# First rows of a fused encoder layer in another fixed order, with three weight casts on GpSimd

## The chip, the cores and the metric

The kernel runs on one core of one Trainium2 chip. The metric is the device time of one launch in microseconds (us), a median over runs. The core's engines have a queue each and work through it in order: TensorE (PE, with its weight loads listed as PEld), VectorE (DVE), ScalarE (ACT), GpSimd (POOL) and SyncE (SP), which issues most of the DMAs.

## The reference

One layer on x (512 rows of 1024 float32): a root-mean-square norm and an input product, two mixers side by side (a state-space scan and a spatial gate), a gated merge, cross-attention to a 256-row memory, and a SwiGLU feed-forward part. What matters here is how it begins:

```python
def rms_norm(x, g):
    xf = x.astype(jnp.float32)
    y = xf * lax.rsqrt(jnp.mean(xf * xf, axis=-1, keepdims=True) + EPS)
    return (y * g.astype(jnp.float32)).astype(x.dtype)
...
        n = rms_norm(h, mix_norm_g[i])
        proj = n @ w_in[i]
        xa = proj[..., :OFF_U]
        zu = proj[..., OFF_U:OFF_V]
        zv = proj[..., OFF_V:OFF_GA]
```

## The kernel before

Every large product is made of three TensorE products. An operand x is split into hi, x rounded to TensorE's float32r format (`F32R`), and lo = x - hi. `mm3` (L421) then accumulates hi times hi, hi times lo and lo times hi into one PSUM bank. So each weight block and each activation costs a cast (the hi half) and a subtraction (the lo half) before it can be multiplied. In most of the kernel `split` (L83) does this, with the cast on ACT and the subtraction on DVE.

The weights come in blocks in a fixed plan. SP loads the raw blocks into three buffers ahead of use. The first product of the kernel is the first half of the columns `zv`: 512 columns, 1024 input rows, in four weight blocks of 256 input rows each. Block w is loaded as `raw[w]`, and its half k is 128 input rows by 512 columns. Blocks 0 and 1 are loaded by two DMAs each, block 2 by one.

The 512 rows of x are four tiles t = 0 to 3 of 128 rows. L640 to L650 load the norm's gain, the two halves of tile 0 (one over ACT's queue, one over SP's), and then over SP's queue weight block 0, tile 1, weight blocks 1 and 2, and tiles 2 and 3.

What follows is the part that the change touches: `first_rows` (L661). It runs a list of steps written out by hand, `ORDER` (L728). Each step issues one instruction, or a small group, and pins it: on each engine, the pinned instructions stand in the order of the list. Instructions of the rest of the kernel that are not pinned are placed between them by a planner, which goes by times that it estimates. A wait in one step holds everything behind it on its engine. The steps, with their first digit the row tile t or the weight block w, are:

- `sq` (ACT): the sum of squares of one half row; the two halves of a row are two steps. `ms` (DVE): the first half's sum divided by D, plus epsilon. `rt` (ACT): the square root over the second half's sum, with `ms` as its bias. `rc` (DVE): the reciprocal.
- `pg` (PE): spreads the gain over the partitions, into PSUM. `sc` (DVE): one half row scaled by the reciprocal and the gain, in place.
- `pt` (PE): four transposes of a half row into PSUM. `hi` (ACT) and `lo` (DVE): the two halves of the transposed row's split.
- `whi` (ACT) and `wlo` (DVE): the split of one half k of weight block w. After `wlo01` the load of weight block 3 is issued (L714).
- `p` (PE): `p` t w k is one `mm3`, three matmuls of 128x512, into the PSUM bank of tile t.
- `idle` (PE): products of a tile of ones that nobody reads.

Half row q = 0 feeds weight blocks 0 and 1, half row q = 1 feeds blocks 2 and 3. `ORDER` has 18 of the 32 products of this stage. What is left of blocks 0 to 2 and the whole of block 3 follow in L1164 to L1177, with four groups of transposes for the state-space part set between them (L785, L793).

Before `ORDER` the kernel issues four idle products and loads ACT's function table for the square root (L634 to L636).

Of the kernel before, what the change touches and what calls it, by code (L numbers as in the profile page):

```python
# [9 lines left out]
F32 = mybir.dt.float32  # L10
# [7 lines left out]
P = 128  # L18
D = 1024
# [5 lines left out]
EPS = 1e-6  # L25
# [27 lines left out]
def hybrid_layer_kernel(  # L53
# [490 lines left out]
    mhalf = cp.tile([P, 9], F32, name="mhalf")[:, 0:1]  # L544
    nc.vector.memset(mhalf, -0.5)

# [107 lines left out]

    def first_products(t, w, k):
        ts = slice(t * P, (t + 1) * P)
        kk = 2 * w + k
        hi, lo = first_w[w]
        mm3(pt[t], (xn_hi[:, kk, ts], xn_lo[:, kk, ts]), (hi[:, k], lo[:, k]), kk == 0, False, turn=pinned[0])

    def first_rows():  # L661

        sums, roots, facs, turned = {}, {}, {}, {}
# [5 lines left out]
        def sq(t, i):  # L669
            if i == 0:  # L670
                sums[t] = np_.tile([P, 2], F32, tag="ss", name="ss", bufs=2)
            j = i if t else 1 - i
            sum_sq(sums[t][:, i:i + 1], xt[:, t, HALF[j]])
# [5 lines left out]
        def rt(t):  # L679
            in_order(nc.scalar.activation(sums[t][:, 0:1], sums[t][:, 1:2], AF.Sqrt, bias=roots.pop(t), scale=1.0 / D))  # L680
# [27 lines left out]

        def wlo(w, k):
            in_order(nc.vector.tensor_tensor(first_w[w][1][:, k], raw[w][:, k], first_w[w][0][:, k].bitcast(F32),  # L710
                                             ALU.subtract))
# [8 lines left out]
        steps = {"pg": pg_, "sq": sq, "ms": ms, "rt": rt, "rc": rc, "sc": sc, "pt": tr, "hi": hi, "lo": lo,  # L720
                 "whi": whi, "wlo": wlo, "p": first_products, "idle": idles, "bank": lambda n: bank3()}
# [1394 lines left out]
```

## Time and profile before

| | |
|---|---|
| time, median of 3 runs | 861.02 us (859.04 to 861.72) |
| the profiled execution's own time | 858.73 us |
| its span, first to last instruction | 857.0 us |
| PE busy | 849.1 us, 99% of the span |
| DVE busy | 667.3 us, 78% |
| ACT busy | 468.5 us, 55% |
| POOL busy | 93.9 us, 11% |
| mean granted TensorE clock | 0.998 |

A row of the timeline has the start in us, the length in us, the engine, the line, the operation, what it writes and reads with shapes, and the number of merged instructions; in brackets stands the idle time of the engine ahead of it and what ended that. Lengths of neighbours overlap, since the next instruction is begun before the last one has quite ended. The distance from start to start is then the price in a queue, and the length is what a waiting engine sees. A row of the windows view has the length of a stretch, each engine's busy time in it, the granted clock, the DMA engines' busy share and GB/s.

### The profile page before, as it was taken

Reading aid. Unit: us, or ns where it says so; the run is one execution under the profiler, and the core shown is the slowest. Engines: PE = TensorE matmul, PEld = TensorE weight load, DVE = VectorE, ACT = ScalarE, POOL = GpSimd, SP = SyncE. Lnnn points to the kernel's source line nnn. Section 1 sums busy time; section 2 is a strip of 40 time slices with the busy share of each in tenths; the row PEclk is TensorE's granted clock in tenths of the full one; section 3 lists DMA queues with packets and bytes.
Section 4 is the critical chain, followed back from the end, with each engine's and each line's share of the span. In section 5 each row is a group of like instructions: output and inputs, shape, how many; then the busy total and the mean of one; then the engine's idle time right before and its main releaser. Section 6 shows DMA issues by size and latency. Waiting matters only on the chain.

```text
span 857.0 us, 14705 instructions
## 1 busy us (share of the span) xinstructions
PE 849.1 (99%) x5736; PEld 763.1 (89%) x5736; DVE 667.3 (78%) x1082; ACT 468.5 (55%) x703; POOL 93.9 (11%) x123
## 2 busy tenths in 40 slices
PE   9999999999999999999999999999999999999997
PEld 6888888888889988899899888999999999988886
DVE  7998798899646767578758755888877768898876
ACT  7835843344455534467457554655545555656674
POOL 0003102111022110120010101002111111000000
PEclk9999999999999999999999999999999999999999
DMA  9879467888475798947686745488989897366564
GB/s 270 222 252 253 130 184 165 223 204 217 125 216 178 243 309 261 306 137 212 220 272 183 180 145 134 145 231 218 239 222 237 216 247 187 102 192 208 194 190 159
DMA packets 119480, 176.37 MB, mean 206 GB/s; under 512 B 9665, under 2 KB 83537, under 8 KB 119250
## 3 DMA queue, kind: packets, MB, share of 16 engines
q1 hardware_dynamic: 96370, 143.13, 50.7%
q0 software_dynamic: 22176, 30.64, 22.1%
q10 hardware_dynamic: 864, 1.66, 0.5%
q8 instruction: 45, 0.74, 0.3%
q14 instruction: 25, 0.20, 0.1%
HBM read 166.52 MB, written 52.92 MB: 256 GB/s over the span
## 4 chain that ended last, share of the span: by engine, by line
PE 95%; DMA 2%; DVE 2%; issue 0%; SPq 0%; ACT 0%; ACTq 0%; DVEq 0%
PE pf L424 22%; PE pt L424 17%; PE px L1316 14%; PE pq L1316 7%; PE dx L424 5%; PE dq L424 5%; PE pv L1316 4%; PE bx L1316 3%; PE qx L1316 3%; PE dv L424 2%; PE pz L1018 2%; PE bq L1316 1%; PE po L424 1%; PE psc L424 1%; PE qq L1316 1%; PE qv L1316 1%
## 5 line engine op out<-in xcount | busy, mean ns | idle before, releaser
L85 ACT CAST whi<-wraw 128x1024 fp32r<-128x1024 f32 (+1 forms) x145 | 149.5, 1031 | 171.4 <-PE pf L424 61.4
L86 DVE TENSOR_TENSOR wlo<-wraw,whi 128x1024 fp32r<-128x1024 f32 (+1 forms) x145 | 173.1, 1195 | 60.7 <-ACT whi L85 59.8
L424 PE MATMUL pf<-xn,whi 128*128 128x512 f32 x448 | 139.2, 391 | 0.0
L424 PEld LDWEIGHTS pf<-xn,whi 128*128 128x128 f32 x448 | 83.7, 188 | 16.8
L1316 PE MATMUL px<-fn,whi 128*128 128x256 f32 x512 | 88.8, 277 | 0.0
L424 PE MATMUL pf<-xn,wlo 128*128 128x512 f32 x224 | 87.7, 392 | 0.0
L1316 PEld LDWEIGHTS px<-fn,whi 128*128 128x128 f32 x512 | 77.3, 188 | 0.2
L1316 PE MATMUL px<-fn,wlo 128*128 128x256 f32 x256 | 70.8, 276 | 0.0
L86 DVE TENSOR_TENSOR wlo<-b,whi 128x1024 fp32r<-128x1024 f32 x39 | 47.7, 1222 | 23.4 <-ACT whi L85 23.4
L85 ACT CAST whi<-b 128x1024 fp32r<-128x1024 f32 x39 | 41.1, 1053 | 41.6 <-PE px L1316 25.5
L1316 PE MATMUL pq<-s,whi 128*128 128x256 f32 x352 | 60.5, 276 | 0.0
L1316 PEld LDWEIGHTS pq<-s,whi 128*128 128x128 f32 x352 | 52.9, 188 | 0.0
L424 PEld LDWEIGHTS pf<-xn,wlo 128*128 128x128 f32 x224 | 42.1, 188 | 8.8 <-issue 0.2
L86 DVE TENSOR_TENSOR wlo<-t,whi 128x1024 fp32r<-128x1024 f32 x30 | 36.7, 1224 | 15.1 <-ACT whi L85 14.9
L1316 PE MATMUL pq<-s,wlo 128*128 128x256 f32 x176 | 48.5, 276 | 0.0
L1316 PEld LDWEIGHTS px<-fn,wlo 128*128 128x128 f32 x256 | 48.1, 188 | 0.0
L85 ACT CAST whi<-t 128x1024 fp32r<-128x1024 f32 x30 | 31.6, 1053 | 30.3 <-DVE t L206 11.2
L424 PE MATMUL pt<-whi,xn 128*128 128x512 f32 x128 | 43.5, 403 | 0.0
L424 PE MATMUL dx<-whi,s 128*128 128x512 f32 x132 | 41.3, 389 | 0.0
L424 PE MATMUL dq<-whi,s 128*128 128x512 f32 x122 | 38.0, 389 | 0.0
L1316 PEld LDWEIGHTS pq<-s,wlo 128*128 128x128 f32 x176 | 33.0, 188 | 0.0
L1316 PE MATMUL px<-s,whi 128*128 128x256 f32 x176 | 30.7, 276 | 0.0
(461 smaller groups left out, 2177.9 us busy)
## 6 DMA issues: line engine op xcount, KB each, us to landing
wraw<-in_w_in_dram SPq DMA_DIRECT2D x34, 512.0 KB, 5.5
dsum<-in_w_down_dram SPq DMA_DIRECT2D x20, 512.0 KB, 6.3
wraw<-dsum SPq DMA_DIRECT2D x20, 512.0 KB, 4.2
b<-in_w_gate_dram SPq DMA_DIRECT2D x15, 512.0 KB, 5.0
wraw<-in_w_down_dram SPq DMA_DIRECT2D x15, 512.0 KB, 3.8
b<-in_w_up_dram SPq DMA_DIRECT2D x14, 512.0 KB, 5.8
dsum<-in_w_down_dram POOLq DMA_DIRECT2D x10, 512.0 KB, 8.2
dsum<-dsum POOLq DMA_DIRECT2D x10, 512.0 KB, 6.2
```

The source lines that it names most:

```text
L85: hi = nc.scalar.copy(dst_hi, src)
L86: lo = nc.vector.tensor_tensor(dst_lo, src, dst_hi.bitcast(F32), ALU.subtract)
L424: m = nc.tensor.matmul(ps, a[x], b[y], start=start and i == 0, stop=stop and i == 2, skip_group_check=free)
L1018: nc.tensor.matmul(ps[:, g, :], wt[:, g, :], u[:, o * GO + g, :], start=True, stop=True)
L1316: m = nc.tensor.matmul(ps[:, j, :], a[x], b[y], start=start and j == k == i == 0, stop=k == 3 and i == 2, skip_group_check=True)
```

## The change

The list of steps is replaced by another list with the same 18 products. Three of the first six weight casts (`01`, `10` and `21`) go from ACT to GpSimd, as a new step `pwhi`. Tiles 1 to 3 have one squaring of the whole row, a new step `sqw`, in place of two of half a row with an `ms`; their square root then takes a constant epsilon as its bias. The squares themselves, which nobody reads, go to a tile `dump`, which takes one of the two buffers that the gains use. The four idle products ahead of the first real product are dropped, and the two ahead of the first transposes stay. Since tile 0 now begins with the product `p001`, the first product into a bank is found by a set rather than by its number. The load of weight block 3 is still issued after `wlo01`.

```diff
-    mhalf = cp.tile([P, 9], F32, name="mhalf")[:, 0:1]
+    small = cp.tile([P, 9], F32, name="small")
+    mhalf, eps = small[:, 0:1], small[:, 1:2]
     nc.vector.memset(mhalf, -0.5)
+    nc.vector.memset(eps, EPS)
...
+    begun = set()
+
     def first_products(t, w, k):
         ts = slice(t * P, (t + 1) * P)
         kk = 2 * w + k
         hi, lo = first_w[w]
-        mm3(pt[t], (xn_hi[:, kk, ts], xn_lo[:, kk, ts]), (hi[:, k], lo[:, k]), kk == 0, False, turn=pinned[0])
+        mm3(pt[t], (xn_hi[:, kk, ts], xn_lo[:, kk, ts]), (hi[:, k], lo[:, k]), t not in begun, False, turn=pinned[0])
+        begun.add(t)
...
-            j = i if t else 1 - i
-            sum_sq(sums[t][:, i:i + 1], xt[:, t, HALF[j]])
+            sum_sq(sums[t][:, i:i + 1], xt[:, t, HALF[1 - i]])
+
+        def sqw(t):
+            sums[t] = np_.tile([P, 2], F32, tag="ss", name="ss", bufs=2)
+            if not dump:
+                dump.append(np_.tile([P, D], F32, tag="gain", name="dump", bufs=2))
+            in_order(nc.scalar.activation(dump[0], xt[:, t], AF.Square, accum_out=sums[t][:, 1:2]))
...
         def rt(t):
-            in_order(nc.scalar.activation(sums[t][:, 0:1], sums[t][:, 1:2], AF.Sqrt, bias=roots.pop(t), scale=1.0 / D))
+            in_order(nc.scalar.activation(sums[t][:, 0:1], sums[t][:, 1:2], AF.Sqrt, bias=roots.pop(t, eps), scale=1.0 / D))
...
+        def pwhi(w, k):
+            in_order(nc.gpsimd.tensor_copy(first_w[w][0][:, k], raw[w][:, k]))
...
     ORDER = """
-        pg0 sq00 sq01 ms0 pg1 rt0 whi00 rc0 sc00 sc01 idle2 pt00 whi01 wlo00 pt01 hi00 hi01 lo00 idle4 sq10 wlo01
-        p000 whi10 ms1 p001 lo01 whi11 wlo10 sq11 wlo11 p010 rt1 whi20 rc1 sc10 p011 whi21 wlo20 pt10 sq20 wlo21
-        p020 hi10 ms2 sq21 lo10 p021 sc11 p100 rt2 sq30 rc2 pt11 sc20 p101 sq31 ms3 sc21 pt20 rt3 p110 hi20 rc3
-        sc30 pt21 hi11 p111 lo20 hi21 pt30 lo11 p200 hi30 lo21 p120 sc31 p201 lo30 pt31 bank3 p300 hi31 p210
-        lo31 p301 p211 p121
+        sq00 pg0 pwhi01 pwhi10 sq01 pg1 ms0 rt0 rc0 sc00 idle2 whi00 pt00 hi00 wlo00 sc01 wlo01 sqw1 rt1 lo00 wlo10 pt01
+        p001 whi11 rc1 sc10 p000 sc11 p010 whi20 pt10 hi01 hi10 wlo11 pt11 pwhi21 lo10 wlo20 sqw2 lo01 rt2 hi11 p011
+        p100 rc2 wlo21 lo11 sqw3 p101 p020 rt3 sc20 p110 p121 rc3 sc30 p111 pt20 hi20 sc21 p021 pt30 hi30 sc31 pt21
+        hi21 lo20 p120 pt31 lo30 p201 lo21 p200 hi31 bank3 p300 p301 p211 lo31 p210
     """
```

More of the change, by code (lines that the diff above doesn't have):

```diff
@@ L658, in first_products @@
         hi, lo = first_w[w]
-        mm3(pt[t], (xn_hi[:, kk, ts], xn_lo[:, kk, ts]), (hi[:, k], lo[:, k]), kk == 0, False, turn=pinned[0])
+        mm3(pt[t], (xn_hi[:, kk, ts], xn_lo[:, kk, ts]), (hi[:, k], lo[:, k]), t not in begun, False, turn=pinned[0])
+        begun.add(t)
     def first_rows():
-        sums, roots, facs, turned = {}, {}, {}, {}
+        sums, roots, facs, turned, dump = {}, {}, {}, {}, []
         raw = [plan[i][3].pop("raw") for i in range(3)]
@@ L718, in bank3 @@
             pt[3] = bank("pt3")
-        steps = {"pg": pg_, "sq": sq, "ms": ms, "rt": rt, "rc": rc, "sc": sc, "pt": tr, "hi": hi, "lo": lo,
-                 "whi": whi, "wlo": wlo, "p": first_products, "idle": idles, "bank": lambda n: bank3()}
+        steps = {"pg": pg_, "sq": sq, "sqw": sqw, "ms": ms, "rt": rt, "rc": rc, "sc": sc, "pt": tr, "hi": hi, "lo": lo,
+                 "whi": whi, "pwhi": pwhi, "wlo": wlo, "p": first_products, "idle": idles, "bank": lambda n: bank3()}
         pinned[0] = True
```

## The prediction

> **What bounds the kernel now.** I read the head of the page first, then the windows, then the timeline of the start.
>
> ```profile
> span 857.0 us, 14705 instructions
> PE 849.1 (99%) x5736; PEld 763.1 (89%) x5736; DVE 667.3 (78%) x1082; ACT 468.5 (55%) x703; POOL 93.9 (11%) x123
> ```
>
> PE is idle for 857.0 - 849.1 = 7.9 us of the span. The windows say where.
>
> ```profile
> 5.00:10.00 5.00, 4.70 (x29) 3.41 (x27) 4.62 (x11) 4.24 (x10) 0.00 (x0) 1.00 0.99 371
> 10.00:15.00 5.00, 4.30 (x20) 3.05 (x21) 4.63 (x11) 4.50 (x13) 0.00 (x0) 1.00 1.05 289
> 15.00:20.00 5.00, 5.00 (x31) 4.26 (x31) 4.87 (x10) 3.57 (x9) 0.00 (x0) 1.00 1.01 239
> 100.00:200.00 100.00, 100.00 (x651) 85.64 (x650) 91.08 (x254) 42.86 (x62) 15.12 (x21) 1.00 0.75 193
> 850.00:857.00 7.00, 1.32 (x12) 1.12 (x10) 2.16 (x6) 2.29 (x7) 0.00 (x0) 0.80 0.39 150
> ```
>
> The columns after the length are PE, PEld, DVE and ACT. Up to 15 us PE waits here and there, then it is full until the tail. So the kernel's time is the moment S from which PE runs without a gap, plus the PE work left at S, plus the tail. Only S and the work done ahead of it can change by this edit. The DVE and ACT columns, 4.6 and 4.2 to 4.5 of 5 us, say that these two engines, which make PE's operands, have hardly any room before 15 us either.
>
> PE's own rows around S, with the idle products at 7.31 (two passes each, so eight rows for four):
>
> ```profile
> 6.20 1.27 PE L694 MATMUL ptr<-ident,xt 128*128 128x128 f32 x8 [0.30 <-DVE pows L819]
> 7.31 1.06 PE L632 MATMUL pt<-ones 128*128 128x128 f32 x8
> 8.13 0.47 PE L424 MATMUL pt<-whi,xn 128*128 128x512 f32 x1
> 10.30 0.50 PE L424 MATMUL pt<-wlo,xn 128*128 128x512 f32 x1 [0.30 <-DVE wlo L710]
> 12.05 0.66 PE L694 MATMUL ptr<-ident,xt 128*128 128x128 f32 x4 [0.31 <-DVE xt L688]
> 14.86 0.63 PE L694 MATMUL ptr<-ident,xt 128*128 128x128 f32 x4
> 16.02 0.60 PE L694 MATMUL ptr<-ident,xt 128*128 128x128 f32 x4
> 21.77 0.27 PE L764 MATMUL plam<-ident,lrows 64*128 64x64 f32 x1
> 25.06 0.61 PE L785 MATMUL pbc<-ident,brow 128*128 128x128 f32 x4
> ```
>
> S is 14.86, at `pt11`. By then 7 of the 18 products of the list are done; 11 products and five groups of transposes (`pt11`, `pt20`, `pt21`, `pt30`, `pt31`) are left. From 14.86 to 16.02 PE does one group and one product: 1.16 us. The 18th product ends at 25.06, where the state-space part's transposes begin, and a small transpose of that part (21.77, 0.2 to the next matmul) stands in between. So 25.06 - 14.86 - 0.2 = 10.0 = 5 x 1.16 + 6 products: a product is 0.70, a group 0.46.
>
> Why S is so late, by the chain of waits, where DMA is a row tile's load:
>
> ```profile
> 4.54 7.51 DMA xt<-in_x_dram
> 12.07 0.72 ACT sq L550 x2
> ...
> 13.37 0.69 DVE xn L703
> ```
>
> Tile 2 lands at 12.05. `hi10`, whose transposes were issued at 12.05, stands behind `sq20` on ACT; `lo10` and `sc11` follow on DVE, and `pt11` waits for `sc11`.
>
> **The change part by part.** Prices of the steps on ACT and DVE:
>
> ```profile
> 5.56 1.29 ACT L707 CAST whi<-wraw 128x512 fp32r<-128x512 f32 x2 [0.55 <-DMA wraw<-in_w_in_dram]
> 8.14 0.63 ACT L550 ACTIVATE sq<-xt 128x512 f32<-128x512 f32 x1
> 10.92 1.12 ACT L707 CAST whi<-wraw 128x512 fp32r<-128x512 f32 x2
> 23.95 1.03 ACT L85 CAST whi<-wraw 128x1024 fp32r<-128x1024 f32 x1
> 5.31 0.75 DVE L688 SCALAR_TENSOR_TENSOR xt<-xt,r,pg 128x512 f32<-128x512 f32 x1
> 7.49 0.69 DVE L703 TENSOR_TENSOR xn<-ptr,xn 128x512 fp32r<-128x512 f32 x1
> 11.05 0.17 DVE L684 RECIPROCAL r<-ss 128x1 f32<-128x1 f32 x1 [0.20 <-ACT ss L680]
> 11.25 0.75 DVE L688 SCALAR_TENSOR_TENSOR xt<-xt,r,pg 128x512 f32<-128x512 f32 x1
> 11.91 1.29 DVE L710 TENSOR_TENSOR wlo<-wraw,whi 128x512 fp32r<-128x512 f32 x2
> ```
>
> On ACT a cast takes 0.62 and its neighbour starts 0.5 later (1.12 for two), a half-row square 0.64 with its read-out. On DVE `rc` takes 0.20 to the next start, `sc` 0.66, and `wlo` 0.61 (1.29 for two of 0.68); I take 0.60 for `lo`.
>
> When data land: the second cast of the pair at 5.56 starts at 5.56 + 1.29 - 0.62 = 6.23, so `raw[0]`'s second half is there by then, and tile 1 by 8.14. For `raw[1]`'s first half, SP's row of its issue and the DMA view of that issue alone (KB, us from issue to landing):
>
> ```profile
> 2.99 1.51 SPq L146 DMA_DIRECT2D wraw<-in_w_in_dram  x3
> wraw<-in_w_in_dram SPq DMA_DIRECT2D x1, 256.0 KB, 5.8
> ```
>
> It lands at 8.79. These loads keep their queue and place, and I leave them where they are.
>
> *The casts on GpSimd* (`pwhi`). The trace has no copy of this size on POOL. Its nearest rows:
>
> ```profile
> 1.49 0.28 POOL masks.py:199 TENSOR_SCALAR_AFFINE_SELECT ident<-ident 128x128 f32<-128x128 f32 x1
> L561 POOL TENSOR_TENSOR r<-ms,mhalf 128x1 f32<-128x1 f32 x10 | 9.1, 910 | 37.9 <-DVE ms L560 37.9
> L886 POOL MEMSET bd<- 128x256 f32 x2 | 0.6, 312 | 0.0
> L2102 POOL MEMSET const-float32-1.0<- 128x1 f32 x1 | 0.1, 104 | 0.0
> ```
>
> From below, twice the memset of 128x256, which reads nothing: 0.62. From the side, the select, which reads and writes: (0.28 - 0.10) / 128 = 1.4 ns per element, so 0.10 + 512 x 0.0014 = 0.82. From above, the same slope on the base of a one-column power, 0.91: 1.63. I take 0.82, since the select is the row that does what a copy does. By the Trainium skill's GPSIMD Engine Reference, section 3.1, a tight loop over 512 elements measured 769 ns; by that, taken as an estimate, the sum below would be 0.05 us better, and no run here shows it yet.
>
> *The new path to S*, step by step. `sc00` ends as before at 6.06. `whi00` (5.56) ends at 6.18, so `wlo00` runs at 6.22 and `sc01` at 6.83; before, `sc01` came first, at 6.06. `pt01` follows `sc01` at 7.6 instead of 6.8. `pwhi01` runs from 6.23 to 7.05; `wlo01` at 7.49, `lo00` at 8.10 to 8.79. `p001`'s first matmul goes at about 8.05 (`p000` went at 8.13), and its last waits 0.3 for `lo00`. Dropping the idle products costs and saves nothing: they ran while PE waited for operands, and this wait remains.
>
> DVE's next step `wlo10` waits for `pwhi10`, which waits for the load: 8.79 + 0.82 = 9.61, `wlo10` at 9.65. Behind it on DVE stand `rc1` (10.26; tile 1's square and root on ACT, 8.14 + 1.05 + 0.3, are done by then), `sc10` (10.46), `sc11` (11.12 to 11.87). On PE `p010`'s second matmul waits for `wlo10` (10.38), `pt10` for `sc10` (11.25), and `pt11` for `sc11`: 11.92. The next, `p011`, has `wlo11` from 11.78 to 12.46 and needs it at about 12.65. So S moves from 14.86 to 11.92, but with only `p001`, `p000` and `p010` done: 15 products are left instead of 11.
>
> Does PE stay full from there? The closest steps on DVE: `lo10` ends at 13.08 and is wanted at 13.5, `lo01` at 14.3 for 14.9, `lo11` at 15.7 for 16.3, `sc20` at 16.3 for 17.2. All arrive, by 0.2 to 0.9 us. Tile 2 (12.05) is no longer ahead of a needed cast: `hi10` stands before `sqw2`.
>
> *One square per row.* The cast of 1024 columns against 512 adds 0.41, so `sqw` is 0.64 + 0.41 = 1.05 in place of two of 0.64, and three `ms` go from DVE. ACT gains 3 x 0.23 and loses three casts of 0.5 to 0.6; none of it ends a wait on the path above, where DVE waits for the load and POOL. I count 0; if ACT were late at `hi10` by more than the 0.4 that `lo10` has spare, it would show there. `eps` is one memset of a column at the start, under the loads: 0. The `dump` tile shares the gains' two buffers; the next tiles there, those of the spatial gate (L1213, L1216), come in the code behind this whole stage: 0. The raw buffers come free as before, so the later loads start as before.
>
> *Sum.* (11.92 - 14.86) + (15 - 11) x 0.70 = -2.94 + 2.80 = -0.14 us. What precedes S moved by almost as much as the work that it used to hold. Against the profiled execution's 858.73 that is 858.6; this execution lies 2.3 us under the median of the three runs, and on the median the forecast is 861.02 - 0.14 = 860.9. Since every 0.1 us more on `pwhi10` moves `wlo10`, `sc11` and S alike, the price of the cast goes straight into the sum: 0.62 gives -0.34, 1.63 gives +0.67.
>
> **The rivals.**
>
> *The GpSimd cast is the new bound (slower).* A row for POOL's one-column power of 0.91 us speaks for a high fixed price per instruction; the memsets of 0.10 and the select of 0.28 speak against it. From 0.96 us per cast the sum is positive: DVE and, behind it, `sc10`, `sc11` and PE wait for `pwhi10`. At 1.63 it is 861.7; to pass +0.3% (2.6 us) the cast would have to take 0.82 + 0.14 + 2.6 = 3.6 us.
>
> *The two engines hold each other up.* No row shows it: POOL has nothing to read at the start. If `pwhi01`, ready at 6.23, and `wlo00`, ready at 6.22, excluded each other, either `pwhi01` would end at 7.72 and `wlo01` run at 7.76 instead of 7.49, which DVE's wait for the load (from 8.70) hides, or `wlo00` would run at 7.10 and `wlo01` at 8.37 to 9.05, and then hold `pwhi10` for 0.26. So 0 to +0.26 beside the sum, 860.9 to 861.1. The Trainium skill's page SBUF — State Buffer, section "SBUF: two separate sides", states such a lock: a DVE instruction with two SBUF inputs and a GpSimd one that reads SBUF do not run together.
>
> *The front shrinks further.* PE's waits ahead of S by my steps are 0.7 for `pt01`, 0.3 in `p001`, 0.3 in `p010`, 0.5 for `pt10` and 0.2 for `pt11`. If the first half of `raw[1]` lands 1 us earlier (tile 1, issued just ahead of it, is there at 8.14) or the cast takes 0.3, then `wlo10` follows `lo00` at 8.75, and `rc1` waits only for tile 1's root, until 9.55 instead of 10.26: -0.7 - 0.14 = -0.8, so 860.2. For it: nothing in this part but this wait is late; against: the issue order of the loads is the same, and DMA is busy 0.99 of the stretch.
>
> *PE's clock falls* with the idle products gone. The first eight idle passes took twice as long as those at 7.31:
>
> ```profile
> 1.06 2.08 PE L632 MATMUL pt<-ones 128*128 128x128 f32 x8 [1.06 <-DVE ones L543]
> 11.00:12.00 1.00, 0.74 (x4) 0.28 (x2) 0.92 (x3) 1.00 (x3) 0.00 (x0) 1.00 0.96 364
> ```
>
> Against it: at 11 to 12 us PE was busy 0.74 and the products after them still went at the 0.70 above. If three products went at twice that, 2.1 more, less the 1.0 of waits that they fill: +1.1 - 0.14 = +1.0, so 862.0.
>
> *The planner sets the rest otherwise*, since its estimated times move: a later load or cast slips behind another on an in-order queue. The closest is block 3:
>
> ```profile
> 25.73 1.23 DVE L86 TENSOR_TENSOR wlo<-wraw,whi 128x1024 fp32r<-128x1024 f32 x1 [0.32 <-issue]
> ```
>
> Its subtraction ends at 26.96. From 25.06 PE has six products of blocks 0 to 2 left (4.2 us), so it is wanted after 29.3 at the earliest: 2.3 us to spare. Either sign, up to 3 us.
>
> **How the numbers follow.** Forecast 0.52, a slow cast 0.16, the lock 0.08, a shorter front 0.12, the clock 0.05, the planner 0.07. A change under 0.3%, 2.6 us, is about what a measurement of this kernel can't tell from none; the three runs before alone span 2.7 us. Only the planner's case passes it by itself, but a median of runs that scatter so can add 1 to 2 us to the outer cases: faster 0.14, same 0.74, slower 0.12. The range takes the cases from -0.8 to +1.0 and the runs' scatter of about 2 us on either side: 858.0 to 863.2.
>
> **What would show it.** In the profile after: a POOL cast of 0.6 to 1.0 us; `wlo10` on DVE at 9.65, right after the second POOL cast; PE's first gapless group at 11.9; then 15 products and five groups, and the 18th product ending within 0.5 us of 24.9. Wrong would be: a first gap of PE after 12.5 us, products more than 0.3 us apart per matmul, a POOL cast above 1.6, or a wait of PE later on that the profile before doesn't have.

## The result, and the profile after

The changed kernel takes 863.09 us (median of 19 runs, 860.09 to 868.1). The kernel before, on the same chip, takes 859.98 us (19 runs, 858.75 to 863.11). The ratio is 1.0028, with a 95% interval of 1.0018 to 1.0039. By the ratio the change made the kernel slower by about 2.4 us; the two medians differ by 3.1 us. The forecast was no change. The profiled execution took 864.44 us, 1.35 us above its median.

The head of its page and two windows of the start (columns as before):

```profile
span 862.6 us, 14678 instructions
PE 850.9 (99%) x5728; PEld 763.9 (89%) x5728; DVE 666.7 (77%) x1080; ACT 465.4 (54%) x694; POOL 96.3 (11%) x126
```

```profile
5.00:10.00 5.00, 3.85 (x21) 2.52 (x19) 4.14 (x10) 3.29 (x7) 1.23 (x2) 1.00 1.00 367
10.00:15.00 5.00, 4.78 (x25) 3.48 (x24) 4.65 (x11) 4.24 (x9) 0.62 (x1) 1.00 0.97 335
```

PE's idle time is 862.6 - 850.9 = 11.7 us, against 7.9 before, and PE was busy 1.8 us more with 8 matmuls fewer. Up to 10 us PE is emptier than before, from 10 us fuller. The front did what it was to do. Its rows in the timeline:

```profile
10.95 1.38 PE L704 MATMUL ptr<-ident,xt 128*128 128x128 f32 x8
12.08 0.48 PE L424 MATMUL pt<-whi,xn 128*128 128x512 f32 x1
24.34 0.27 PE L776 MATMUL plam<-ident,lrows 64*128 64x64 f32 x1
9.35 0.69 DVE L723 TENSOR_TENSOR wlo<-wraw,whi 128x512 fp32r<-128x512 f32 x1 [0.59 <-POOL whi L720]
6.81 0.61 POOL L720 CAST whi<-wraw 128x512 fp32r<-128x512 f32 x1 [5.03 <-DMA wraw<-in_w_in_dram]
8.70 0.62 POOL L720 CAST whi<-wraw 128x512 fp32r<-128x512 f32 x1 [1.28 <-DMA wraw<-in_w_in_dram]
```

`pt10` and `pt11` are the eight transposes at 10.95. This view merges them; in the trace the first transpose of `pt11` starts at 11.70, 0.38 us ahead of the product at 12.08: that is S. The same matmul stands 0.43 us earlier than before all the way from 28 to 90 us.

Where is the time lost, then? The table gives how much later the same matmul of PE starts than in the profile before (median over 5 us from the time at the head), then the median of the runs, that of the kernel before on the same chip, and the ratio of the two. The kernels are those of the experiments below; `before_again` and `after_again` are further runs of the two kernels themselves.

```
                  28     100    400    420    470    520    545   median  before  ratio [95%]
before_again     +0.35  +0.35  +0.35  +0.47  +2.05  +2.05  +2.05  860.92  860.63  1.0008 [0.9997, 1.0018]
before_root2     +0.37  +0.37  +0.37  +0.54  +0.54  +0.54  +0.54  859.44  860.60  0.9992 [0.9980, 1.0004]
before_lam_ctrl  +0.47  +0.42  +0.47  +0.50  +2.07  +2.07  +2.07  860.52  860.45  1.0004 [0.9993, 1.0016]
before_lam_late  +0.47  +2.05  +2.12  +2.03  +2.07  +2.07  +2.07  861.43  860.45  1.0010 [1.0002, 1.0019]
after            -0.43  +1.92  +1.97  +2.29  +3.86  +3.87  +5.61  863.09  859.98  1.0028 [1.0018, 1.0039]
after_again      -0.29  +2.15  +2.19  +2.76  +2.76  +2.76  +5.36  864.03  860.45  1.0041 [1.0021, 1.0060]
after_root2      -0.22  +1.93  +1.97  +2.81  +2.81  +2.81  +2.81  861.97  860.60  1.0024 [1.0008, 1.0041]
after_keep1      +0.01  +0.64  +0.65  +0.63  +0.63  +0.63  +2.44  861.67  859.98  1.0022 [1.0010, 1.0034]
keep1_root2      +0.34  +3.57  +3.57  +3.17  +4.74  +4.74  +4.74  859.96  859.98  1.0012 [0.9993, 1.0032]
after_pow0       +0.71  +0.67  +0.72  +0.51  +2.08  +2.08  +2.42  860.42  860.38  1.0000 [0.9989, 1.0012]
pow0_root2       -0.12  +0.11  +0.16  +0.22  +1.79  +1.80  +1.80  860.47  860.38  0.9993 [0.9983, 1.0003]
lam_early        +0.18  +0.10  +0.10  +0.02  +0.06  +0.06  +1.45  860.40  860.45  1.0004 [0.9991, 1.0018]
lam_keep_late    +0.60  +3.57  +3.57  +3.49  +3.52  +3.53  +5.12  862.16  859.98  1.0029 [1.0017, 1.0041]
lam_act          +1.15  +1.13  +1.13  +1.11  +1.11  +1.11  +1.51  861.38  860.63  1.0007 [0.9994, 1.0021]
lam_sq           +1.24  +1.16  +1.16  +1.08  +1.11  +1.12  +1.12  860.50  860.63  0.9998 [0.9987, 1.0009]
lam_exp          +0.43  +0.38  +0.37  +0.57  +0.57  +0.57  +1.82  859.75  860.63  0.9991 [0.9980, 1.0003]
exp_root2        +0.45  +0.39  +0.38  -0.01  -0.01  -0.00  -0.00  859.67  860.60  0.9992 [0.9981, 1.0003]
```

In the changed kernel's profile two losses belong to the change: 2.4 us between 95 and 99 us (-0.46 at 90, +1.92 at 100), and 1.7 us at 527 us. The 1.6 us between 420 and 470 us do not: they are in one of the two profiles of the changed kernel and in one of the two of the kernel before. A third and smaller loss, 0.3 to 0.8 us between 400 and 420 us, stands in the three profiles `after`, `after_again` and `after_root2`, where PE waits for a `wlo` near 408 us; it is at most 0.2 us in all others, `after_pow0` among them, and was not followed. The view of PE's waits from 20 us to the tail, which is empty for the kernel before, names the places (the last row is the one near 408 us):

```profile
PE ptr L587 <- DVE xs L578: 1.5, 1, 1.5
PE pw L1023 <- DVE zh L1036: 1.1, 1, 1.1
PE pz L1030 <- ACT wt L1024: 0.5, 1, 0.5
PE pt L424 <- DVE wlo L86: 0.4, 1, 0.4
```

**The first loss.** `pw` and `pz` belong to the state-space part, `zt` and the one-column powers to the spatial gate's norm. After, in the order of the chain:

```profile
86.34 0.15 DVE L1219 TENSOR_SCALAR ms<-ms 128x1 f32<-128x1 f32 x1
82.38 1.18 POOL L336 DMA_DIRECT2D bsum<-in_w_proj_b_dram  x1 [7.72 <-DMA bsum<-in_w_proj_b_dram]
88.33 1.17 POOL L336 DMA_DIRECT2D bsum<-in_w_proj_b_dram  x1 [4.77 <-DMA bsum<-in_w_proj_b_dram]
89.00 1.12 POOL L1220 TENSOR_TENSOR r<-ms,small 128x1 f32<-128x1 f32 x1
90.15 0.16 DVE L1221 TENSOR_TENSOR nm<-nm,r 128x1 f32<-128x1 f32 x1 [2.40 <-POOL r L1220]
90.34 1.25 ACT L1222 ACTIVATE zt<-zt,nm,r 128x1024 f32<-128x1024 f32 x1 [2.48 <-DVE nm L1221]
93.00 0.58 ACT L1024 COPY wt<-pw 128x512 f32<-128x512 f32 x1
93.48 1.25 ACT L1222 ACTIVATE zt<-zt,nm,r 128x1024 f32<-128x1024 f32 x1
94.62 0.58 ACT L1024 COPY wt<-pw 128x512 f32<-128x512 f32 x1
96.51 1.04 ACT L1035 COPY zh<-pz 64x512 f32<-64x512 f32 x1
97.58 1.02 DVE L1036 COPY zh<-pz 64x512 f32<-64x512 f32 x1 [0.58 <-ACT zh L1035]
98.66 0.66 PE L1023 MATMUL pw<-ident,wsx 128*128 128x128 f32 x4 [1.12 <-DVE zh L1036]
```

Before, GpSimd's rows of the same stretch:

```profile
78.50 1.18 POOL L336 DMA_DIRECT2D bsum<-in_w_proj_b_dram  x1 [4.70 <-DMA bsum<-in_w_proj_b_dram]
80.75 0.56 POOL L1208 TENSOR_TENSOR r<-ms,mhalf 128x1 f32<-128x1 f32 x1 [1.07 <-DVE ms L1207]
84.17 1.19 POOL L336 DMA_DIRECT2D bsum<-in_w_proj_b_dram  x1 [2.85 <-DMA bsum<-in_w_proj_b_dram]
```

Before, the gate's first power stands between two accumulating loads of `bsum` on GpSimd's in-order queue. After, it stands behind the second one, which waits for its plain load and starts at 88.33. The power's operand was there at 86.34 + 0.15 = 86.5, but it runs at 89.00, 2.5 us later. Its normalization goes to ACT at 90.34, after 2.48 us of idle time, and ACT's queue behind it is late: the second `wt` copy, then `zh`, then DVE's half of `zh`, for which PE waits.

The load itself also comes 4.2 us later than before (88.33 against 84.17), since SP issues its plain load 4.1 us later. On SP's in-order queue that load stands behind stores of what the state-space part has made (`kd<-ks`), and these are as much later. Before, then after:

```profile
75.18 1.83 SPq L970 DMA_DIRECT2D kd<-ks  x4
77.54 1.17 SPq L335 DMA_DIRECT2D bsum<-in_w_proj_b_dram  x1
```

```profile
79.26 1.84 SPq L982 DMA_DIRECT2D kd<-ks  x4
81.64 0.56 SPq L335 DMA_DIRECT2D bsum<-in_w_proj_b_dram  x1
```

So SP's queue carries lateness to GpSimd too. This is read from the rows, and no edit tested it alone; in `before_lam_ctrl`, which loses nothing here, the load is issued at 80.90.

**The second loss** is the same pattern, with the accumulating load of `t` (L199). After, then before:

```profile
528.52 0.15 DVE L562 TENSOR_SCALAR ms<-ms 128x1 f32<-128x1 f32 x1
529.96 1.32 POOL L199 DMA_DIRECT2D t<-in_w_gate_dram  x1 [4.53 <-ACT full L597]
530.80 1.06 POOL L563 TENSOR_TENSOR r<-ms,small 128x1 f32<-128x1 f32 x1
531.90 1.42 DVE L578 SCALAR_TENSOR_TENSOR xs<-h,r,g_f 128x512 f32<-128x512 f32 x2 [3.23 <-POOL r L563]
```

```profile
523.28 1.32 POOL L199 DMA_DIRECT2D t<-in_w_gate_dram  x1 [1.73 <-issue]
524.96 0.56 POOL L561 TENSOR_TENSOR r<-ms,mhalf 128x1 f32<-128x1 f32 x1 [0.35 <-DVE ms L560]
```

Here the order on GpSimd is the same in both kernels, but after, the accumulating load starts later than the power's operand is ready (528.52 + 0.15), and the power follows it by 0.84 us. Before, the load was there 1.68 us ahead of the power, so it had 1.68 - 0.84 = 0.84 us to spare. The row names ACT's `full` as what ended the load's wait, but it cannot be: in the kernel before the load ran at 523.28, ahead of ACT's `full` of that row tile:

```profile
524.84 1.07 ACT L595 COPY full<-ptr 128x512 f32<-128x512 f32 x2 [0.42 <-PE ptr L585]
```

The semaphore events of the trace show the rest. GpSimd's queue ends its wait for the plain load of `t` (and for a semaphore of PE, which had come earlier), and the accumulating load starts 1.2 us behind that in every profile. These are the times, the first less PE's shift at 518 us, beside what PE lost at 527 us:

```
                 wait over  load starts  second power  wait over less shift  lost at 527
before             522.06     523.28       524.96            522.06            0.00
before_again       524.58     525.81       527.01            522.53            0.00
before_lam_ctrl    524.70     525.92       527.03            522.63            0.00
before_lam_late    524.82     526.05       527.03            522.75            0.00
lam_sq             524.23     525.46       526.30            523.11            0.00
after_pow0         525.51     526.74       527.59            523.43            0.33
lam_act            524.62     525.84       526.69            523.51            0.40
lam_exp            524.93     526.16       527.00            524.36            1.25
lam_early          524.57     525.80       526.65            524.51            1.39
lam_keep_late      528.23      529.46       530.31            524.70            1.59
after              528.73     529.96       530.80            524.87            1.75
after_keep1        525.55      526.78       527.63            524.92            1.81
after_again        528.48     529.71       530.56            525.72            2.60
```

Up to 523.1 nothing is lost, and beyond that nearly each us of lateness is one of PE.

### The profile page after: what moved, and what is told of

Read it like the earlier page. It is cut to its first block, busy times and chain, and to the rows that moved or that the text cites. A ratio compares the mean times of both kernels' runs of the same rounds, so it can differ in the third digit from the quotient of the medians.

```text
span 862.6 us, 14678 instructions
## 1 busy us (share of the span) xinstructions
PE 850.9 (99%) x5728; PEld 763.9 (89%) x5728; DVE 666.7 (77%) x1080; ACT 465.4 (54%) x694; POOL 96.3 (11%) x126
## 4 chain that ended last, share of the span: by engine, by line
PE 88%; DVE 5%; DMA 3%; issue 2%; ACT 1%; POOL 1%; SPq 0%; POOLq 0%; DVEq 0%
PE pf L424 21%; PE px L1328 14%; PE pt L424 13%; PE pq L1328 7%; PE dx L424 5%; PE dq L424 5%; PE pv L1328 3%; PE bx L1328 3%; PE qx L1328 3%; PE dv L424 2%; DMA ed<-e 2%; PE qq L1328 1%; PE psc L424 1%; PE qv L1328 1%; PE bq L1328 1%
```

## The experiments

**Is it the lambda transpose?** The transpose `plam` opens the setup of the state-space part, and no step of the list pins it. Before, the planner put it between two products at 21.77. After, it stands behind the list's last product at 24.34, and DVE, which takes the result over, is idle until 24.21:

```profile
24.21 1.23 DVE L86 TENSOR_TENSOR wlo<-wraw,whi 128x1024 fp32r<-128x1024 f32 x1 [2.58 <-ACT whi L85]
25.36 0.22 DVE L778 COPY slab<-plam 128x64 f32<-128x64 f32 x1
```

In the kernel before that copy ran at 22.08, and the chain behind it began at 23.58 instead of 25.61. First theory (A): this delay reaches PE at 95 us. Four kernels, the first being the changed kernel once more. The others pin the transpose and the copy by a new step `lam0`, which also issues the transpose's loads:

```diff
+    def lam(n):
...
+        in_order(nc.tensor.transpose(ps.rearrange("p i g -> p (i g)"), lrows.rearrange("r d p -> r (d p)"), ident[:2 * G, :2 * G]))
+        lr, li = small(), small()
+        in_order(nc.vector.tensor_copy(slab[:, used[0] - 2:used[0], :], ps))
```

`lam_early` has the changed list with `p300 lam0 p301`, `before_lam_late` the old list with `lam0` at its end, and `before_lam_ctrl` the old list with `p300 lam0 hi31`, one matmul behind the planner's place.

> The changed kernel once more, for which of its losses come back. Theory A (a late state-space setup: the small transpose plam now stands behind all 18 products of the list, at 24.3 us instead of 21.8, so VectorE's chain of state-space work starts later and PE waits for it between 60 and 100 us): the loss of about 2.4 us there comes back in the trace, the time is 2 to 3.5 us over the kernel before. The further losses of the first profile (0.3 at 408 us, 1.6 from slower products between 424 and 465, 1.7 at 528 where GpSimd is held) are of that one execution and stay away. Theory B (these later losses belong to the new order of the whole program): they come back too, with about the same sizes.

> The changed kernel, with the loads, the transpose and the copy of plam as a pinned step of the list, behind p300 (PE at about 21.3 us). Theory A: VectorE's state-space chain starts at about 22.5 instead of 25.6 us, PE's wait near 95 to 99 us goes, the time is 0.3 to 1 us under the kernel before. Theory B or C (C: the front of the new list itself costs the time): 2 to 3 us over the kernel before, as the changed kernel.

> The kernel before with its old list, and plam pinned behind the list's last product (PE at about 25 us instead of 21.8). Theory A: 1.5 to 3 us over the kernel before, lost between 60 and 140 us, with no other part of the change in it. Theory B or C: within 0.5 us of the kernel before.

> The control for pinning as such: the kernel before with plam pinned one matmul later than where the planner had put it. All theories: within 0.7 us of the kernel before.

Measured: the changed kernel lost both again in `after_again`, 2.5 us at 95 to 99 us and 2.6 us at 527, but nothing between 424 and 465 us. With the early transpose the changed list loses nothing at 95 to 99 us (+0.18 at 28, +0.10 at 100), and its time is that of the kernel before (1.0004, 0.9991 to 1.0018). With the late transpose the old list loses 1.6 us there (+0.47 to +2.05), and its median is 1 us up. The control loses nothing there. The waits of PE in `before_lam_late`:

```profile
PE pw L1017 <- DVE zh L1030: 1.3, 1, 1.3
```

So the place of the transpose makes the first loss, in either list. `lam_early` still lost 1.4 us at 527 us. How a transpose at 24 us reaches PE 70 us later was not told by these four.

**Which part of the front matters?** Three kernels on top of `lam_early`, and the kernel before once more. `lam_act` puts the three casts back on ACT, behind `hi00`, `rt1` and `hi10`. `lam_sq` has half-row squares with `ms`, and `idle4` ahead of `pt01`. `lam_exp` moves `lam0` further ahead and pins the exponential of the setup as a step `exp0`:

```diff
-        sq00 pg0 pwhi01 pwhi10 sq01 pg1 ms0 rt0 rc0 sc00 idle2 whi00 pt00 hi00 wlo00 sc01 wlo01 sqw1 rt1 lo00 wlo10 pt01
+        sq00 pg0 sq01 pg1 ms0 rt0 rc0 sc00 idle2 whi00 pt00 hi00 whi01 wlo00 sc01 wlo01 sqw1 rt1 lo00 whi10 wlo10 pt01
...
-        sq00 pg0 pwhi01 pwhi10 sq01 pg1 ms0 rt0 rc0 sc00 idle2 whi00 pt00 hi00 wlo00 sc01 wlo01 sqw1 rt1 lo00 wlo10 pt01
+        sq00 pg0 pwhi01 pwhi10 sq01 pg1 ms0 rt0 rc0 sc00 idle2 whi00 pt00 hi00 wlo00 sc01 wlo01 sq10 ms1 sq11 rt1 lo00 idle4 wlo10 pt01
...
-        p100 rc2 wlo21 lo11 sqw3 p101 p020 rt3 sc20 p110 p121 rc3 sc30 p111 pt20 hi20 sc21 p021 pt30 hi30 sc31 pt21
-        hi21 lo20 p120 pt31 lo30 p201 lo21 p200 hi31 bank3 p300 lam0 p301 p211 lo31 p210
+        p100 rc2 wlo21 lo11 sqw3 p101 p020 rt3 exp0 sc20 p110 p121 rc3 sc30 p111 pt20 hi20 sc21 p021 pt30 hi30 sc31 pt21
+        hi21 lo20 p120 lam0 pt31 lo30 p201 lo21 p200 hi31 bank3 p300 p301 p211 lo31 p210
```

> The repaired list (plam pinned behind p300), with the three casts 01, 10 and 21 back on ScalarE behind hi00, rt1 and whi20. By the rows of the changed kernel a GpSimd cast takes 0.61 and the second one lets wlo10 run at 9.35; on ScalarE whi10 stands behind rt1 (9.5) and ends at 10.1, so wlo10, sc11 and S come about 0.8 us later: 0.5 to 0.8 us over the repaired list. If the casts bring nothing, equal to it within 0.3 us.

> The repaired list, with two half-row squares and the first half's sum per row, and with the four idle products, as before. The prediction counts both edits at 0: within 0.4 us of the repaired list, S of the front the same within 0.4 us in the trace. If one square per row matters, ScalarE is late at hi10 or at the third and fourth rows and PE waits there: 0.5 us or more over it.

> The repaired list, with plam one product group earlier (ahead of pt31, at about 20 us) and ScalarE's table load and exponential pinned behind rt3, where ScalarE idles 2 us in the changed kernel. Theory A (VectorE's state-space chain is the second bound of the stretch up to 140 us): the chain starts near 21 to 22 us instead of 23 to 24; since PE no longer waits for it at 95 us in the repaired list, the time is equal to the repaired list or up to 0.4 us under it.

> The kernel before once more, for a second trace of it: the first one, 858.7 us, lies under its median. If the hold of GpSimd near 527 us (the plain load of t lands 8 to 11 us after its issue, the accumulating load on GpSimd's queue waits for it, and the root behind that) is of the changed list, it is absent here and PE's shift against the first trace stays under 0.7 us to the end. If it comes and goes with the transfers of an execution, a wait of 1 us or more can show here too.

Measured: without the casts on GpSimd the front is 1.0 us later (+1.15 against +0.18), with `wlo10` at 10.91 against 9.95, behind ACT's cast. Some 0.3 us of that is not the casts': PE ran at half speed up to 7.3 us there (the idle passes at 6.34 took 1.06 us, in `lam_early` 0.61), so `hi00` and ACT's queue behind it were late, down to the square of tile 1 (8.89 against 8.60). The rest, about 0.7, is near the 0.8 that was expected. The time does not show it (1.0007 against 1.0004). `lam_sq` shows +1.24, but there too PE itself was slow: the trace's clock record begins at 9.18 us, against 4.55 in `lam_early`, and the first transposes took 1.06 us instead of 0.63. The idle products ahead of `pt01` ran in that stretch and held it to 9.64, against 7.76 in `lam_early`:

```profile
7.49 1.06 PE L726 MATMUL ptr<-ident,xt 128*128 128x128 f32 x4
9.64 0.60 PE L726 MATMUL ptr<-ident,xt 128*128 128x128 f32 x4
```

What the squares cost is therefore not settled. (The second raw half landed late as well, its cast started at 9.92 against 9.30, but PE did not wait for it.) In both kernels the windows view gives 1.00 for that stretch, ahead of the first clock record, so it does not tell this. `lam_exp` is the fastest of these, 0.9991, but its interval (0.9980 to 1.0003) reaches 1. The kernel before, profiled again, has its front 0.35 us later than its first profile, and the 1.6 us between 420 and 470 us.

**The accumulating load of `t`** (theory B). In three kernels it is set behind the second power of the block, the one it held, instead of the first: in the changed kernel, in `lam_exp` and in the kernel before.

```diff
-                    behind(add, powers[-NT])
+                    behind(add, powers[1 - NT])
```

> The changed kernel with one edit: GpSimd's accumulating load of t (L199) stands behind the second one-column power of the block's four instead of behind the first. In the profile after, that load waited for the plain load of t and held the second power from about 525 to 530.80, and PE then waited 1.5 us for xs. If this hold is a term of the loss (theory B, beside the late lambda transpose), PE no longer waits for xs at 527-531 and the shift of PE's rows against the profile before stays at what it is at 500 us (about +1.9 to +2.8, the transpose's part): about 1.4 us less than after, 861.5 to 862.8. If the hold is only a symptom (the load of t itself is late and something behind it would wait as long), PE waits elsewhere between 527 and 560 and the time stays at 863 to 864.

> The kernel lam_exp (changed list, lambda transpose and its exponential in their early places) with the same edit of the accumulating load. Theory B: the +1.25 us that lam_exp's PE lost at 527 goes, 859.75 - 1.25 = 858.5 (857.8 to 859.3), faster than the kernel before by 1 to 2 us. Rival (the load is late anyway): 859.5 to 860.5, PE waiting after 527 us for an operand made from t.

> The kernel before with the same edit: in its profile the load of t had landed before GpSimd issued the accumulating one (523.28), the second power ran at 524.96 and no wait of PE followed. Theory B: no difference, within 0.5 us of the kernel before, PE without a wait at 527. If the accumulating load, now about 2 us later, is itself on a path, PE waits between 530 and 560 us and it is 0.5 to 2 us slower.

Measured: nothing is lost at 527 us any more (+2.81 at 520 and 545 in `after_root2`, +0.00 in `exp_root2`), and no wait of PE appears behind it. In `after_root2`:

```profile
527.75 0.55 POOL L563 TENSOR_TENSOR r<-ms,small 128x1 f32<-128x1 f32 x1 [3.38 <-DVE ms L562]
529.07 1.32 POOL L199 DMA_DIRECT2D t<-in_w_gate_dram  x1 [0.77 <-ACT full L597]
```

So in the traces the hold is what PE's wait at 527 us comes from. In the run times that is not clear of noise. In the changed kernel the median with the edit is 1.4 us over the kernel before's, where without it the changed kernel was 3.1 and 3.6 over, but the intervals of the ratios overlap (1.0024, 1.0008 to 1.0041, against 1.0028, 1.0018 to 1.0039). On top of `lam_exp` the trace gained 1.8 us, but the median nothing (859.67 against 859.75): 858.5 was expected, a miss, and the hold does not cost its full length in every execution of that kernel. In the old kernel the edit makes no difference that the interval can tell.

**How the late transpose reaches PE.** Over the last dozen instructions ahead of the gate's first normalization, ACT's order is the same with the early and with the late transpose. From there the changed kernel has normalization, `wt`, normalization, `wt`, two squares, `zh`, where `lam_early` has both normalizations, both `wt`, `zh`, then the squares. So a second theory (A2) was that this order is what costs, against the delay itself (A1). `after_keep1` orders the changed kernel's ACT, and `keep1_root2` adds the edit of B. `lam_keep_late` does the opposite to `lam_early`'s squares:

```diff
+            if t == 2:
+                behind(sq, keeps[1])
...
+        if t == 1:
+            behind(norm, gate[5])
```

> The changed kernel, its lambda transpose still late, with ScalarE's order at 93 to 97 us as in lam_early: the second wt copy ahead of the normalization of row tile 1 (L1222), and the zh copy (L1035) ahead of the squares of row tile 2. Theory A1 (the late transpose delays the state-space chain on VectorE by some 3 us, and the delay itself reaches PE): PE still waits for zh or wt between 93 and 105 us, about 1.6 us, and the shift of PE's rows at 100 us stays near +1.9. Theory A2 (the delay alone would be absorbed; what costs is that the planner, given the late transpose, puts a normalization and two squares ahead of wt and zh on ScalarE's in-order queue): no wait there, and the shift at 100 us stays at the front's -0.2 to -0.5. The hold at 527 us stays in both: 863.1 - 2.4 = 860.7 by A2, 862.5 to 863.5 by A1.

> The kernel lam_early (lambda transpose early, no wait of PE at 95 to 99 us) with two squares of row tile 2 (1.4 us) put ahead of the zh copy on ScalarE, as they stand in the changed kernel; nothing else is late. Theory A2: VectorE's zh copy, which ended at 96.46 in lam_early, ends about 97.9, and PE's second four pw transposes, at about 97.3, wait for it by 0.3 to 0.8 us: shift at 100 us +0.5 to +1.0 against +0.10 in lam_early. Theory A1: no wait there, shift within 0.2 of lam_early's. Time within 0.7 us of lam_early's 860.4 either way.

> The changed kernel with both repairs of order and nothing else: ScalarE's order at 93 to 97 us as in after_keep1, and GpSimd's accumulating load of t behind the second power as in after_root2. If these two orders are the whole loss (A2 and B), PE keeps the front's gain to the end: a shift of -0.2 to -0.5 at 100 us and 0 to +0.7 after 540 us (some 0.5 is lost at 406 us in several of these kernels), span 856.7 to 857.7, and a median 0.5 to 1.5 us under the kernel before. If A1 holds, +1.9 at 100 us and a median about 1 us above it.

Measured: neither theory as it stood, but ACT's order counts. `after_keep1` lost 0.7 us at 95 to 99 us, not 2.4, though its first normalization started as late as in the changed kernel (90.47 against 90.34). `lam_keep_late` lost 3.0 where at most 0.9 was expected, with its normalization at 90.88 after 3.97 us of idle time. `keep1_root2`, with `after_keep1`'s order there, lost 3.3 us in its profile. But that execution took 863.58 us, and the median of this kernel, 859.96, is that of the kernel before. (`after_keep1` also lost 1.5 us between 700 and 800 us, waiting for weights of `dq`; that place was not followed.)

About half of the losses of `keep1_root2` and `lam_keep_late` is not a wait. PE waited there for 1.34 us (for `wt`) and 1.24 us (for `zh`). Behind that the granted clock was 0.50 for 3.41 us, from 97.02 and from 99.23 us, and the 128x512 matmuls stood 0.43 us apart instead of 0.23. In `keep1_root2`, the wait and the window around it, with a mean clock of 0.70:

```profile
95.71 2.51 PE L1032 MATMUL pz<-u,wt 128*128 128x64 f32 x16 [1.34 <-ACT wt L1026]
```

```profile
95.00:100.00 5.00, 4.29 (x22) 3.89 (x23) 3.79 (x6) 5.00 (x11) 0.00 (x0) 0.70 0.88 244
```

In the other profiles the clock stays at 1.00 from its first record to the tail, in the changed kernel's with its waits too. Between the two profiles with one order of ACT, what moved with the wait was GpSimd's second accumulating load of `bsum`, here in `keep1_root2` (in `after_keep1` it started at 88.46):

```profile
90.41 1.17 POOL L336 DMA_DIRECT2D bsum<-in_w_proj_b_dram  x1 [5.75 <-DMA bsum<-in_w_proj_b_dram]
91.07 1.12 POOL L1224 TENSOR_TENSOR r<-ms,small 128x1 f32<-128x1 f32 x1
```

Theory C follows: the late transpose makes the planner put the gate's first power behind that load, and the loss comes from that. The orders fit in part. In `before_lam_late` and all kernels with the changed kernel's loss the power is behind it, in `before_lam_ctrl`, `lam_exp` and the kernel before ahead of it. `lam_early`, `lam_act` and `lam_sq` have it behind the load as well (in `lam_early` it was held from 84.86 to 88.21), but with ACT's other order, and lose nothing there. So the held power alone does not cost PE anything; with the changed kernel's order of ACT it may. To test C, `after_pow0` moves that one load and leaves ACT's order as in the changed kernel, and `pow0_root2` adds the edit of B:

```diff
+            adds.append(nc.gpsimd.dma_start(d, x, accum_op=ALU.add))
...
+        if t == 0:
+            pow0.append(power)
+            if len(adds) >= 4:
+                behind(adds[4 - 1], power)
```

> The changed kernel, lambda transpose late, ScalarE's order as in the changed kernel; on GpSimd the one-column power of the spatial gate's row tile 0 (L1220 there) stands ahead of the second accumulating load of bsum, as it does in the kernel before, where the changed kernel has it behind. In the changed kernel this power's operand was ready at 86.5 us, but it ran at 89.00, behind the load that waited until 88.33 for its plain load; in after_keep1 the normalization behind it still started at 90.47. Theory C (this hold of about 2.4 us on GpSimd is what PE's waits at 95 to 99 us come from): the power runs at about 86.7, the normalization at about 88, and the waits for wt and zh go or shrink to under 0.4 us; shift at 100 us -0.3 to +0.3; the hold at 527 us stays (+1.4 to +2.6): median 860.5 to 861.5. Theory A1 or A2 (the delay of the chain, or ScalarE's order alone): PE's waits stay above 1 us and the shift at 100 us stays at +1.5 to +2.2.

> The changed kernel with both of GpSimd's accumulating loads behind the power that they held (bsum as in after_pow0, t as in after_root2), and nothing else. If the two holds are the whole loss (theories C and B), PE's shift stays between -0.5 and +0.7 from the front to the tail, span 856.5 to 857.7, and the median is 0 to 1.2 us under the kernel before's of the same chip. If not, a wait of PE above 1 us remains between 90 and 130 us.

Measured, GpSimd in `after_pow0`, where PE waits for nothing between 20 us and the tail that the view names:

```profile
82.55 1.18 POOL L322 DMA_DIRECT2D bsum<-in_w_proj_b_dram  x1 [7.12 <-DMA bsum<-in_w_proj_b_dram]
87.32 1.54 POOL L1227 TENSOR_TENSOR r<-ms,small 128x1 f32<-128x1 f32 x1 [3.59 <-DVE ms L1226]
89.00 1.19 POOL L322 DMA_DIRECT2D bsum<-in_w_proj_b_dram  x1
```

The loss at 95 to 99 us is gone (+0.71 at 28, +0.67 at 100), with the transpose still late and ACT's order unchanged; 0.33 us are still lost at 527. So the loss at 95 to 99 us needs both orders: GpSimd's, with the power behind the load, and ACT's, with a normalization and the squares ahead of `wt` and `zh`. (With ACT's order alone put right, in `after_keep1`, 0.7 us of it stayed.) The time is that of the kernel before (1.0000, 0.9989 to 1.0012). With both edits PE's shift is -0.12 at 28 us and +0.22 at 420, there is no loss at 527, and the ratio is 0.9993 (0.9983 to 1.0003). So moving the two loads takes the whole loss away. In the run times the load of `bsum` alone does that already; what the load of `t` adds is seen in the traces alone. No kernel of the study is clearly faster than the kernel before; the best three (`lam_exp`, `exp_root2` and `before_root2`) are at 0.9991 and 0.9992, with intervals that reach 1.

## Why the prediction was wrong

*S and the sum of the front: right, within what a profile can tell.* S came at 11.70 against 11.92, and `wlo10` at 9.35 against 9.65, 0.03 behind the end of the second GpSimd cast at 9.32. The difference of 0.3 at `wlo10` is the cast's: 0.62 and started at 8.70, against 0.82 from 8.79. That is the lower bound of the range given for it, 0.62, for which the text said -0.34. With S at 11.70 the sum would be (11.70 - 14.86) + 4 x 0.70 = -0.36. (By the rows a group takes 0.38 and the product behind it 0.78, not 0.46 and 0.70; only their sum, 1.16, enters.) The front's shift was -0.43 in the first pair of profiles. Over the seven profiles with the changed list, and no step of the list touched, it is -0.43 to +0.71, mean 0.00; over the five with the old list, the first at 0, it is 0 to +0.47, mean +0.33. So the front gains about 0.3 us, with a scatter of a single profile that is larger. "15 products are left instead of 11" holds, and the shift from 28 to 90 us stays at -0.43 to -0.46, so PE did stay full behind the front.

*The step that failed* is the first one: "So the kernel's time is the moment S from which PE runs without a gap, plus the PE work left at S, plus the tail. Only S and the work done ahead of it can change by this edit." PE was full after 15 us in the profile before, but nothing was said of the slack with which it was full. The list pins only its own steps. Everything unpinned that shares a queue with it, the transpose `plam` first, is placed anew. The rival "the planner sets the rest otherwise" was the right one. It was given 0.07 and up to 3 us "either sign", and it was judged by one place, block 3's subtraction, which came earlier after the change (24.21 against 25.73) and cost nothing. The place that decided was on GpSimd, 60 us later, together with ACT's order behind it. The rows that would have told of it are in the profile before: the accumulating load at 84.17, waiting 2.85 us for a DMA between two powers, and the load at 523.28 with 0.84 us to spare.

*"The later loads start as before"* is wrong. The second plain load of `bsum` was issued at 81.64 instead of 77.54, behind the state-space part's stores on SP's queue. That of `t` was issued at the same distance from PE's matmuls as before (at 513.37 with the shift taken off, against 513.25), but landed 11.4 us after its issue instead of 8.7. Both are waited for on GpSimd's queue, and their landing now decides PE's waits. Counted from PE's shift, the wait for `t` was over between 522.06 and 522.75 in the four profiles with the old list and between 523.11 and 525.72 in the nine with a form of the changed one, in the table above. With the edit of B the load landed, counted in the same way, at 522.6 in the old list and between 522.5 and 524.2 in the four kernels with a form of the changed one. So the later landing is a tendency of the changed list and not a rule. Why stays open: no run separated that.

*The rivals on the front.* The slow GpSimd cast fell: 0.61 or 0.62. The two engines' holding each other up was real. In `lam_exp` it cost nothing on the path, as said: the stretched cast ended at 7.71, ahead of the subtraction that needs it (7.87). In the changed kernel the first cast starts at 6.81, where the subtraction `wlo00` (6.15, 0.69) ends. Where the two overlap, one is stretched. First `lam_exp`, where the cast takes 1.08, then `lam_sq`, where the subtraction takes 0.91:

```profile
6.63 1.08 POOL L747 CAST whi<-wraw 128x512 fp32r<-128x512 f32 x1 [4.85 <-DMA wraw<-in_w_in_dram]
6.55 0.68 DVE L750 TENSOR_TENSOR wlo<-wraw,whi 128x512 fp32r<-128x512 f32 x1
```

```profile
6.35 0.61 POOL L742 CAST whi<-wraw 128x512 fp32r<-128x512 f32 x1 [4.57 <-DMA wraw<-in_w_in_dram]
6.59 0.91 DVE L745 TENSOR_TENSOR wlo<-wraw,whi 128x512 fp32r<-128x512 f32 x1
```

In either case the one that started first kept its usual time, and the other ended 0.48 and 0.54 us after it (7.71 against 7.23, and 7.50 against 6.96), where it takes 0.61 and 0.68 alone. Five more profiles show the same: four have casts of 0.69 to 1.13 us that end 0.46 or 0.47 behind the subtraction, and `keep1_root2` a subtraction of 1.08 us that ends 0.55 behind the cast. By the Trainium skill's page SBUF — State Buffer, section "SBUF: two separate sides", whichever of the two starts first gets the shared port for the whole instruction; these rows agree but for the 0.13 and 0.14 us by which the second is shorter than its usual length. PE's clock did not fall in the front: in none of the profiles without the four idle products does it leave 1.00 between its first record and 90 us. One square per row was counted at 0; `lam_sq` did not settle it.

*The size.* The range, 858.0 to 863.2, held the median, but only by its upper end, and the chance of slower was given as 0.12. That it held was luck, since none of the cases that it was built from came. By its own terms, 862.0 plus about 2 us, the upper end would have been 864.0. The statement of what would be wrong, "a wait of PE later on that the profile before doesn't have", is what came.

## What to carry to other kernels

An edit of a hand-written order moves more than the pinned steps: go through every unpinned chain that starts within it, and compare each engine's order, SP's and GpSimd's too and not only PE's, far behind the edit. On an in-order queue look for a small operation behind one that waits for a transfer: here a 0.55 us power behind an accumulating load cost up to 2.4 and 1.7 us of PE. "PE is full" says nothing of the slack; write down by how much each such wait is covered, since the cover is what a shift of 2 us uses up.

## What the runs showed of the hardware that was not expected

The same 128x256 products between 424 and 465 us start 113 ns apart in some executions and 118 ns in others, of either kernel, at a granted clock of 1.00; their lengths in the records, which overlap, are 276 and 281 ns. That is worth 1.6 us, about two thirds of the effect studied. Kernel before, in its first profile and again, from the groups of that window (busy time, mean ns of one):

```profile
L1316 PE MATMUL qx<-hn,whi 128*128 128x256 f32 x92 | 15.9, 276 | 0.0
```

```profile
L1316 PE MATMUL qx<-hn,whi 128*128 128x256 f32 x81 | 14.6, 281 | 0.0
```

What sets it was not tried. Another surprise is how far a load's landing moves from one execution to the next. In `after_keep1` and `keep1_root2`, which have the same order there, the second accumulating load of `bsum` started at 88.46 and 90.41, with PE 0.3 us apart. About half of that is the issue of its plain load (81.59 and 82.54), the rest is the way from there.

The third is the clock. The fall to 0.50 for 3.41 us behind a wait of PE, in `keep1_root2` and `lam_keep_late`, shows in the mean clock of a run as well. Of the 12 runs of `keep1_root2` the four longest, 863.58 to 866.71, have 0.995 to 0.997, and the other eight, 858.43 to 860.29, have 0.998 or more. Of the 19 of the changed kernel 865.08 and 868.1 have 0.996 and 0.995, and in `after_again` the four from 866.43 on have 0.995. Runs below 0.998 occur in six kernels, all with the gate's power behind the load of `bsum`, and not in `lam_exp`, `after_pow0` or `pow0_root2` (858.48 to 861.33); of the 137 runs of the kernel before on these chips one is below (864.38 us, 0.997). That the held power, by way of PE's wait, makes these long runs fits, but was not tested; waits of up to 2.4 us in other profiles left the clock at 1.00.
